# Seven block products in place of eight in the feed-forward layers of a three-layer fp32 stack

## The chip, the core and the metric

The kernel runs on one core of a Trainium2 chip. The metric is device time in microseconds (us) from the start to the end of one execution. Engines are named as in the profile: PE does matrix products (PEld is its weight load), DVE, ACT and POOL work on tiles elementwise, SP issues DMAs.

## The reference

512 tokens of width 1024 go through three layers in fp32. Two hybrid layers mix attention, a convolution and retention, and a third layer mixes differential attention with a state-space model. Each layer ends in a feed-forward part, and these are what is changed:

```
# hybrid layers (two of them): w_up 1024 x 4096, w_down 4096 x 1024
h = rms_norm(x, g_mlp_pre)
f = jnp.square(jax.nn.relu(h @ w_up)) @ w_down
x = x + rms_norm(f, g_mlp_post)
# last layer: w_up 1024 x 5632, w_down 2816 x 1024, conv of three tokens on each column
gate, val = split(causal_dwconv(h @ w_up), 2)
x = x + (silu(gate) * val) @ w_down
```

## The kernel before, in words

**Products.** PE has fp32r operands, so each fp32 operand is split in a high part (rounded to fp32r) and a low part (the rest), and each product is three matmuls: high x high, high x low, low x high (`mm3`, line 863; `t_part`, line 911). The high part of a weight chunk is a copy (`nc.copy`, ACT, or DVE at a planned penalty), the low part a subtraction (`nc.sub`, DVE or POOL).

**Weights** stream from memory in the order of `stream_spec` (line 60) in chunks of 128 x 1024 (512 KB). `Stream.load_to` loads a chunk into one of 4 raw slots (pool `wr`, tile wraw), and `prep_to` (line 748) makes the tiles whi and wlo of it in one of 4 slots each. `take` (line 766) hands a chunk to the products that use it. Preparation is wanted 15 us before use (`PREPV`).

**Feed-forward before.** The normed input lies transposed in hhi, hlo (features on partitions, 512 tokens as columns). The up projection makes one block of 128 hidden features per chunk: 8 x 3 matmuls with 512 columns (`f_unit`, line 890); the first four blocks of a layer are made in two halves of 256 tokens (`f_split`, line 896), since the second half of the input is still being normed. `relu2` (in `mlp`, line 1444), or the convolution and Silu (in `ffn2`, line 2006), takes each block out of PSUM and splits it in fhi, flo. The down projection (`down`, line 1483) takes four blocks of features at a time: for each half of the 1024 outputs it uses two chunks, for each of four tiles of 128 tokens 4 x 3 matmuls with 512 columns into one PSUM bank, which DVE adds to the accumulator acc (or to X in the last layer). Down group g-1 follows up group g. `finish_mlp` (line 1504) does the last group and the norms.

**Order.** The kernel records every instruction with the time by which it is wanted, and a planner (class `Trace`, line 400) orders them before anything runs, with a cost for each (`cost`, line 682: 1.04 ns a column and 65 ns for a DVE tensor_tensor, 2.1 ns a column and 150 ns for one on POOL). It simulates the engines as independent of each other. Where an instruction may go on two engines, it goes on the one where cost plus a bias ends first; in the feed-forward parts POOL's bias is -1000 ns (`wbias` 3). On the chip each engine then runs its list in that order. All instructions are issued by line 642, which is why the profile shows this line everywhere; they are told apart by their tiles. In the first feed-forward part a side task (`ssm_params`, line 1525) computes parameters of the third layer on POOL and DVE.

```python
    BIAS = [2000.0, 100000.0, -4449.0, -1000.0]                       # line 404
    def sub(self, out, a, b, bias=1):                                 # line 648
        alts = [("vector", "tensor_tensor", None)]
        if all(v.t.pool.space == "SB" for v in (out, a, b)):
            alts.append(("gpsimd", "tensor_tensor", bias))
```

PSUM has 4 banks for main products (`psp`) and 4 for side tasks (`pss`).

Of the kernel before, what the change touches and what calls it, by code (L numbers as in the profile page):

```python
# [46 lines left out]
def mlp_groups():  # L47
    return [(4 * g, 4) for g in range(NG1)]


def ffn2_groups():
    n = DFF2 // 128
    return [(k, min(4, n - k)) for k in range(0, n, 4)]
# [6 lines left out]
def stream_spec():  # L60
    out = []
    for l in range(LAYERS):
        for m in range(2):
            out.append(f_chunk("w_in", l, C_CONV + 128 * m))
            out.append(f_chunk("w_in", l, C_CONV + 256 + 128 * m))
        for c in (C_RV, C_RQ, C_RK, C_AV):
            out += t_chunks("w_in", l, ((c, 384),))
        for p in range(3):
            out.append(f_chunk("w_in", l, C_AQ + 128 * p))
            out.append(f_chunk("w_in", l, C_AK + 128 * p))  # L70
        for p in range(3):
# [3 lines left out]
        gs = mlp_groups()  # L75
        for g, (k0, n) in enumerate(gs):
            out += [f_chunk("w_up", l, 128 * (k0 + i)) for i in range(n)]
            if g:
                out += down_chunks("w_down", l, *gs[g - 1])
        out += down_chunks("w_down", l, *gs[-1])  # L80
# [19 lines left out]
    gs = ffn2_groups()  # L100
    for g, (k0, n) in enumerate(gs):
        for i in range(n):
            out.append(f_chunk("w_up_2", 0, 128 * (k0 + i)))
            out.append(f_chunk("w_up_2", 0, DFF2 + 128 * (k0 + i)))
        if g:
            out += down_chunks("w_down_2", 0, *gs[g - 1])
    out += down_chunks("w_down_2", 0, *gs[-1])
# [117 lines left out]
class View:  # L225
    """A view of a tile that is traced before the tile is placed."""
# [47 lines left out]
    def mask(self):  # L274
        """First and last column, and which ones between unless it's all."""
# [54 lines left out]
class DramView(View):  # L330
    """A view of a tile in DRAM: taken as a whole."""
# [20 lines left out]
class Pool:  # L352
    """Equal slots, which the order of instructions deals out to tiles. Each is a pool of one buffer."""
# [46 lines left out]
class Trace:  # L400
    """Records instructions with the time by which each is wanted, orders them, and issues them."""
# [246 lines left out]
    def sub(self, out, a, b, bias=1):  # L648
# [3 lines left out]
        return self.add(alts, (out, a, b), {"op": ALU.subtract})  # L652
# [119 lines left out]

class Side:
# [35 lines left out]
class Builder:  # L809
# [3 lines left out]
    NR, NW = 4, 4  # L813
# [6 lines left out]
    def __init__(self, tc, ctx, A, out):  # L820
# [17 lines left out]
        self.wbias = 2  # L838

# [23 lines left out]
    def mm3(self, ps, w, a, start, stop):  # L863
        nc = self.nc
        (whi, wlo), (ahi, alo) = w, a
        nc.tensor.matmul(ps, whi, ahi, start=start, stop=False)
        nc.tensor.matmul(ps, whi, alo, start=False, stop=False)
        nc.tensor.matmul(ps, wlo, ahi, start=False, stop=stop)
        self.tick(3 * ahi.n * 0.422)
# [72 lines left out]
    # ---------------------------------------------------------------- norms  # L942
# [42 lines left out]
    def to_hT(self, t, hs):  # L985
        nc = self.nc
        for h in range(2):
# [4 lines left out]
            self.split(ps.rearrange("p (k n) -> p k n", k=4), self.hhi[sl], self.hlo[sl])  # L992
# [66 lines left out]
    # ---------------------------------------------------------------- attention helpers  # L1059
# [41 lines left out]
    def v_pack(self, src):  # L1101
        """V of six heads, each as 64 columns of high parts and 64 of low parts."""
# [11 lines left out]
    def pv_pair(self, h, pts, V, y):  # L1114
        """One head's output, from the products with the high and the low parts of V below each other."""
# [19 lines left out]
    def rows(self, third):  # L1135
        """Room for the four rows of blocks of a lower triangle."""
# [3 lines left out]
    def p_split(self, parts):  # L1140
        """High and low parts by blocks of keys: 512, 384 and twice 256 columns, the last with a block of zeros."""
# [58 lines left out]
    # ---------------------------------------------------------------- conv module  # L1200
# [48 lines left out]
    # ---------------------------------------------------------------- retention  # L1249
# [87 lines left out]
    # ---------------------------------------------------------------- hybrid layer  # L1337
    def hybrid(self, l):
# [69 lines left out]
        # output projection and residual  # L1408
# [14 lines left out]
        self.side.drain()  # L1423
        self.finish(lambda t: (p0[t],), 4, W_OUT_KS, mix, X, gpost, gpre)
# [18 lines left out]
    # ---------------------------------------------------------------- MLP  # L1443
    def mlp(self, l, X):
        nc = self.nc
        groups = mlp_groups()
# [3 lines left out]
        acc = [None] * NT  # L1450
        f = {}
        last_g = len(groups) - 1

        def relu2(m):
            def ev(ps):
                r = self.s2()
                nc.vector.tensor_scalar(r, ps, 0.0, None, op0=ALU.max)
                hi, lo = self.s2(F32R, "fhi"), self.s2(F32R, "flo")
                nc.scalar.activation(hi, r, AF.Square)
                nc.scalar.activation(r, r, AF.Square)  # L1460
                nc.vector.tensor_tensor(lo, r, hi.bitcast(F32), op=ALU.subtract)
                f[m] = (hi, lo)
            return ev
        lhs = lambda k, t0, t1: tuple(z[:, t0:t1] for z in f[k])
        for g, (k0, n) in enumerate(groups):
            if g == 0:
                self.f_split([relu2(i) for i in range(n)], self.mid_start((1, 3)))
                gpost = self.load_gain(4 * l + 3)
                nxt = 4 * (l + 1) if l + 1 < LAYERS else 8
                gpre = self.load_gain(nxt)  # L1470
            else:
                for i in range(n):
                    self.f_unit(relu2(k0 + i))
                self.down(groups[g - 1], lhs, acc, f, g == 1)
        xd = [[self.dp.tile(F32, f"xd{l}_{t}_{h}", [P, 512]) for h in range(2)] for t in range(NT)]

        def store(t):
            for h in range(2):
                nc.sync.dma_start(out=xd[t][h], in_=X[t][h])
        self.finish_mlp(groups[-1], lhs, acc, X, gpost, gpre, store)  # L1480
        self.xd = xd

    def down(self, grp, lhs, acc, f, first):
        nc = self.nc
        k0, n = grp
        nch = n // 2
        ks = list(range(k0, k0 + n))
        for h in range(2):
            ws = [self.ws.take() for _ in range(nch)]
            for t in range(NT):  # L1490
                ps = self.ps()
                for c in range(nch):
                    self.t_part(ps, ws[c], ks[2 * c:2 * c + 2], t, 512, lhs, c == 0, c == nch - 1)
                if first:
                    if h == 0:
                        acc[t] = [None, None]
                    acc[t][h] = self.s2(name="acc")
                    nc.scalar.copy(acc[t][h], ps)
                else:
                    nc.vector.tensor_tensor(acc[t][h], ps, acc[t][h], op=ALU.add)  # L1500
        for k in ks:
            f.pop(k)

    def finish_mlp(self, grp, lhs, acc, X, gpost, gpre, store):
        nc = self.nc
        k0, n = grp
        nch = n // 2
        ks = list(range(k0, k0 + n))
        ws = [self.ws.take() for _ in range(2 * nch)]
        hs = {}  # L1510
        for t in range(NT):
            for h in range(2):
                ps = self.ps()
                for c in range(nch):
                    self.t_part(ps, ws[h * nch + c], ks[2 * c:2 * c + 2], t, 512, lhs, c == 0, c == nch - 1)
                nc.vector.tensor_tensor(acc[t][h], ps, acc[t][h], op=ALU.add)
            self.post_update(t, acc[t], X, gpost)
# [3 lines left out]
            store(t)  # L1521
        self.pending = hs

    # ---------------------------------------------------------------- SSM parameters
# [158 lines left out]
    # ---------------------------------------------------------------- SSM  # L1683
# [84 lines left out]
    # ---------------------------------------------------------------- differential attention  # L1768
# [84 lines left out]
    def second(self):  # L1853
# [139 lines left out]
        hs = {}  # L1993
        for t in range(NT):
# [11 lines left out]
    def ffn2(self, X):  # L2006
        nc = self.nc
        f, tg = {}, {}
        self.wbias = 3
        cw, cb = PV["convw2"][0], PV["convb2"][0]  # L2010

        def unit(i, val):
            c = i + (22 if val else 0)

            def ev(ps):
                t = self.s2(name="cv")
                w = [self.pvt[:, cw + 3 * c + j:cw + 3 * c + j + 1] for j in range(3)]
                nc.scalar.activation(t, ps, AF.Identity, scale=w[2], bias=self.pvt[:, cb + c:cb + c + 1])
                nc.vector.scalar_tensor_tensor(t[:, 1:], ps[:, :511], w[1], t[:, 1:], op0=ALU.mult, op1=ALU.add)
                nc.vector.scalar_tensor_tensor(t[:, 2:], ps[:, :510], w[0], t[:, 2:], op0=ALU.mult, op1=ALU.add)  # L2020
                if not val:
                    nc.scalar.activation(t, t, AF.Silu)
                    tg[i] = t
                else:
                    g = tg.pop(i)
                    nc.vector.tensor_tensor(t, t, g, op=ALU.mult)
                    hi, lo = self.s2(F32R, "fhi"), self.s2(F32R, "flo")
                    self.split(t, hi, lo)
                    f[i] = (hi, lo)
            return ev  # L2030
        lhs = lambda k, t0, t1: tuple(z[:, t0:t1] for z in f[k])
        groups = ffn2_groups()
# [47 lines left out]
```

## Time and profile before

| | |
|---|---|
| time, median of 3 runs | 2184.35 us (2183.29 to 2185.64) |
| span of the profiled execution, first to last instruction, which is its own time | 2185.0 us |
| PE busy | 2065.8 us (95%) |
| DVE, ACT, POOL busy | 1395.2, 928.5, 745.5 us |
| moved from and to memory | 204.25 MB read, 19.14 MB written |

Busy time of an engine is the union of its instructions; a waiting instruction that has already started counts as busy. Matmuls overlap in the records, so their distance in time from start to start is the price of one, not their duration. The same holds for DVE: one instruction's end overlaps the next one's start by about 0.1 us.

### The profile page before, as it was taken

To read this page: it belongs to the slowest core of one execution; us is meant where nothing else is said; L and a number is where in the kernel's file an instruction comes from. 1 tells how busy PE (TensorE), PEld (TensorE's weight loads), DVE (VectorE), ACT (ScalarE), POOL (GpSimd) and SP (SyncE) were. 2 spreads that over 40 slices of the span, in tenths; PEclk is the share of its full clock that TensorE was granted. 3 is DMA by queue.
4 is the path that set the end of the run, shared out by engine and by line. 5 is a ranking of instruction groups with operands and counts; after the bars stand their busy time and mean duration, and the time that the engine had idled before them with its cause. 6 is when DMAs were issued, how large, how long until landed. Compare 5 with 4: busy or idle time off the path is not lost. (4 is left out here: it accounts for less than half of the span.)

```text
span 2185.0 us, 27033 instructions
## 1 busy us (share of the span) xinstructions
PE 2065.8 (95%) x9964; PEld 1711.6 (78%) x9964; DVE 1395.2 (64%) x2131; ACT 928.5 (42%) x1521; POOL 745.5 (34%) x858
## 2 busy tenths in 40 slices
PE   7789989899999799989999998999999999999999
PEld 7777878778888777788888877677777788888887
DVE  6999596344457999573444464379888646655545
ACT  3267544232234267454222344456578324433332
POOL 3663357980004663210000115764643431000000
PEclk9999999999999999999999999999999999999999
DMA  5223233332333224133332346222224533333222
GB/s 176 80 78 123 87 116 109 128 127 87 97 114 97 87 68 135 49 107 97 96 97 77 115 133 201 79 80 68 92 82 135 169 96 97 97 96 97 87 87 77
DMA packets 85556, 225.16 MB, mean 103 GB/s; under 512 B 10416, under 2 KB 20400, under 8 KB 85424
## 3 DMA queue, kind: packets, MB, share of 16 engines
q1 hardware_dynamic: 85424, 223.43, 32.4%
q8 instruction: 79, 1.29, 0.3%
q14 instruction: 53, 0.43, 0.1%
HBM read 204.25 MB, written 19.14 MB: 102 GB/s over the span
## 5 line engine op out<-in xcount | busy, mean ns | idle before, releaser
L642 POOL TENSOR_TENSOR wlo<-wraw,whi 128x1024 fp32r<-128x1024 f32 (+1 forms) x156 | 374.5, 2408 | 1068.3 <-ACT whi L642 824.9
L642 ACT CAST whi<-wraw 128x1024 fp32r<-128x1024 f32 (+1 forms) x323 | 330.4, 1029 | 726.7 <-PE ps L642 592.1
L642 PE MATMUL ps<-hhi,whi 128*128 128x512 f32 (+1 forms) x1488 | 506.8, 370 | 7.3 <-DVE acc L642 3.1
L642 PE MATMUL ps<-hlo,whi 128*128 128x512 f32 (+1 forms) x1488 | 504.8, 370 | 5.6 <-DVE hlo L642 5.6
L642 PE MATMUL ps<-hhi,wlo 128*128 128x512 f32 (+1 forms) x1488 | 504.3, 369 | 0.3 <-DVE wlo L642 0.3
L642 PEld LDWEIGHTS ps<-hhi,whi 128*128 128x128 f32 x1488 | 272.4, 191 | 54.8 <-issue 4.0
L642 PEld LDWEIGHTS ps<-hlo,whi 128*128 128x128 f32 x1488 | 272.4, 191 | 53.5 <-DVE hlo L642 6.8
L642 PEld LDWEIGHTS ps<-hhi,wlo 128*128 128x128 f32 x1488 | 272.1, 191 | 48.2 <-DVE wlo L642 1.0
L642 DVE TENSOR_TENSOR wlo<-wraw,whi 128x1024 fp32r<-128x1024 f32 x178 | 223.4, 1257 | 114.8 <-ACT whi L642 114.5
L642 PE MATMUL ps<-whi,fhi 128*128 128x512 f32 x688 | 249.7, 392 | 6.1 <-DVE t L642 3.7
L642 PE MATMUL ps<-whi,flo 128*128 128x512 f32 x688 | 249.5, 391 | 0.0
L642 PE MATMUL ps<-wlo,fhi 128*128 128x512 f32 x688 | 249.5, 391 | 0.0
L642 PE MATMUL ps<-wlo,hhi 128*128 128x384 f32 (+1 forms) x448 | 162.7, 380 | 18.3 <-POOL wlo L642 18.1
L642 DVE TENSOR_TENSOR acc<-ps,acc 128x512 f32<-128x512 f32 x112 | 76.5, 687 | 154.7 <-PE ps L642 154.7
L642 PE MATMUL ps<-whi,hhi 128*128 128x384 f32 (+1 forms) x448 | 161.7, 383 | 14.2 <-DVE rotb L642 12.7
L642 PE MATMUL ps<-whi,hlo 128*128 128x384 f32 (+1 forms) x448 | 158.8, 377 | 0.0
L642 PEld LDWEIGHTS ps<-whi,fhi 128*128 128x128 f32 x688 | 129.6, 189 | 34.7 <-DVE t L642 4.2
L642 PEld LDWEIGHTS ps<-wlo,fhi 128*128 128x128 f32 x688 | 129.6, 189 | 27.8
L642 PEld LDWEIGHTS ps<-whi,flo 128*128 128x128 f32 x688 | 129.5, 188 | 27.8
L642 DVE SCALAR_TENSOR_TENSOR cacc<-cy,pv,cacc 128x509 f32<-128x509 f32 (+26 forms) x120 | 125.3, 1088 | 0.6
L642 POOL TENSOR_TENSOR st<-st,mhalf 128x1 f32<-128x1 f32 (+1 forms) x56 | 54.9, 981 | 194.4 <-DVE st L642 190.8
L642 PEld LDWEIGHTS ps<-wlo,hhi 128*128 128x128 f32 x448 | 86.9, 195 | 30.6 <-POOL wlo L642 21.6
(250 smaller groups left out, 3167.8 us busy)
## 6 DMA issues: line engine op xcount, KB each, us to landing
wraw<-in_wst SPq DMA_DIRECT2D x302, 512.0 KB, 3.5
wraw<-in_wst SPq DMA_DIRECT2D x32, 384.0 KB, 3.1
gain<-in_gains SPq DMA_DIRECT2D x20, 256.0 KB, 4.2
X<-in_x SPq DMA_DIRECT2D x16, 256.0 KB, 6.1
xd<-X SPq DMA_DIRECT2D x16, 256.0 KB, 2.0
X<-xd SPq DMA_DIRECT2D x16, 256.0 KB, 4.9
gated<-t SPq DMA_DIRECT2D x16, 256.0 KB, 2.4
gate<-gated SPq DMA_DIRECT2D x16, 256.0 KB, 3.7
```

The lines of the kernel that those rows point to most:

```text
L642: getattr(getattr(self.nc, e), m)(*[r(x) for x in op.args], **{k: r(v) for k, v in op.kw.items()})
```

## The change

In each feed-forward part, all but the first four feature blocks of the up projection and the last group of the down projection are computed by 2 x 2 blocks with seven block products (Strassen's algorithm in Winograd's form). Tokens are cut in halves of 256, the inner dimension and the outputs in halves too. A unit takes two chunks x, y of 128 x 1024, and makes 84 matmuls of 256 columns (7 products of 4 x 3). Before, two chunks made 48 matmuls of 512 columns.

- The sums of weight blocks are made on chip: `take_fast` makes four sums of 512 columns (into a third raw slot, tile wsum, in place of y, and into a tile of the common pool) and splits 3.5 chunks instead of 2.
- The sums of the activations are made on chip: `fast_in` once a layer for the input, `fast_mid` for each pair of hidden feature blocks.
- The block products are combined by `FastUp.out` and `FastDown.out`, as they leave PSUM. Each unit uses two PSUM banks; products 4 and 3 of a unit run within the next unit.
- X is written to memory before the layer and read back at its end. whi and wlo get 5 slots each in place of 4, the common pool 51 tiles of 128 x 512 in place of 55.

There are 14 up and 14 down units in each hybrid layer, and 20 up and 10 down units in the last, 86 in all. The planner, its costs and its biases are as before.

```diff
+    def take_fast(self):
+        x, y = self.raw.pop(j), self.raw.pop(j + 1)
+        t0 = b.T - b.PREPV
...
+        b.prio(t0)
+        split(x, (1, 2))
+        b.prio(t0 + 3 * b.PROD)
+        z, z4 = b.wr.tile(name="wsum"), b.s2(name="wsum")
+        nc.sum(z[:, L], x[:, L], y[:, L], b.wbias)
+        nc.sum(z[:, R], z[:, L], y[:, R], b.wbias)
+        split(z, (5, 6))
+        b.prio(t0 + 6 * b.PROD)
+        nc.sum(y[:, L], y[:, L], y[:, R], b.wbias)
+        nc.sum(z4, z[:, R], x[:, R], b.wbias)
+        split(y, (7, 3))
+        b.prio(t0 + 8 * b.PROD)
+        split(z4, (4,))
...
+    def fast_mid(self, g0, g1, s4, e):
+        sa = self.s2(name="sraw")
+        nc.sub(sa[:, R], g0[:, R], g1[:, R], self.wbias)
+        nc.sub(sa[:, L], sa[:, R], g0[:, L], self.wbias)
+        nc.sum(s4[0][:, H], g1[:, L], sa[:, L], self.wbias)
+        nc.sub(g0[:, R], g0[:, L], g0[:, R], self.wbias)
+        for src, names in ((g0, (1, 7)), (g1, (2, 4)), (sa, (6, 5))):
+            hi, lo = self.s2(F32R, "fhi"), self.s2(F32R, "flo")
+            nc.copy(hi, src)
+            nc.sub(lo, src, hi.bitcast(F32), self.wbias)
...
+        hi, lo = s4[1][:, H], s4[2][:, H]
+        nc.copy(hi, s4[0][:, H])
+        nc.sub(lo, s4[0][:, H], hi.bitcast(F32), self.wbias)
...
+class FastUp(Fast):
+    def out(self, i):
+        pa, pb = self.pa[:, :256], self.pb[:, :256]
+        if i == 1:
+            nc.copy(m0[:, L], pa)
+        elif i == 2:
+            nc.vector.tensor_tensor(g0[:, L], pb, m0[:, L], op=ALU.add)
+        elif i == 6:
+            nc.copy(m0[:, R], pa)
+        elif i == 7:
+            nc.copy(m1[:, L], pa)
+            nc.vector.tensor_tensor(g1[:, R], pb, m1[:, L], op=ALU.subtract)
+        elif i == 4:
+            nc.copy(g0[:, R], pa)
+            self.done(0, g0)
+        elif i == 3:
+            nc.vector.tensor_tensor(g1[:, L], pb, m0[:, R], op=ALU.subtract)
+            self.done(1, g1)
...
+class FastDown(Fast):
+    def out(self, i):
+        if i in (1, 6, 7):
+            m = b.s2(name="mid")
+            nc.copy(m, pa)
...
+                nc.sub(C[1, 1], C[1, 1], m, b.wbias)
+        elif i == 2:
...
+                V(C[0, 0], pb, C[0, 0], op=ALU.add)
+                nc.sum(C[0, 0], C[0, 0], self.m1, b.wbias)
+        elif i == 5:
+                V(C[1, 1], pb, C[1, 1], op=ALU.add)
+        elif i == 4:
+                V(C[1, 0], pa, C[1, 0], op=ALU.add)
+        elif i == 3:
+                V(C[0, 1], pb, C[0, 1], op=ALU.add)
+                nc.sub(C[0, 1], C[0, 1], self.mu, b.wbias)
...
-    NR, NW = 4, 4
+    NR, NW = 4, 5
+    PROD = 1300
...
+    def fast_unit(self, u):
+        for i in (1, 2, -4, 6, -3, 5, 7):
...
+        def done(j):
+            def d(e, g):
+                nc.vector.scalar_tensor_tensor(g, g, 0.0, g, op0=ALU.max, op1=ALU.mult)
```

In the last layer `conv(i, val, src)` reads the combined block from SBUF, where it read PSUM before, with the same instructions.

## Rows read from the trace of the kernel before

**Rows 1.** The page: its head, and the first of its busy lines.
```profile
span 2185.0 us, 27033 instructions
PE 2065.8 (95%) x9964; PEld 1711.6 (78%) x9964; DVE 1395.2 (64%) x2131; ACT 928.5 (42%) x1521; POOL 745.5 (34%) x858
```
**Rows 2.** The chain that ended last: start us, us, what (of six pieces one).
```profile
1819.57 361.70 PE ps L642 x1640
```
**Rows 3.** Busy by stretch: stretch us, its length, engines' busy us, PEclk, DMA share, GB/s.
```profile
50.00:100.00 50.00, 37.21 (x189) 35.17 (x188) 49.96 (x68) 8.80 (x16) 27.25 (x19) 0.90 0.26 82
985.00:1250.00 265.00, 265.00 (x1153) 216.28 (x1153) 116.81 (x130) 83.51 (x104) 16.67 (x8) 1.00 0.31 93
1860.00:2150.00 290.00, 290.00 (x1255) 235.57 (x1255) 158.22 (x190) 100.73 (x126) 9.66 (x4) 1.00 0.30 95
```
**Rows 4.** Timeline of PE in the second layer's f_split: start us, us, instruction.
```profile
962.02 0.28 PE L642 MATMUL ps<-hhi,wlo 128*128 128x256 f32 x1
...
963.38 0.28 PE L642 MATMUL ps<-hhi,wlo 128*128 128x256 f32 x1
```
**Rows 5.** Timeline of PE in the second layer's down projection.
```profile
1046.11 0.39 PE L642 MATMUL ps<-whi,fhi 128*128 128x512 f32 x1
...
1047.47 0.39 PE L642 MATMUL ps<-whi,fhi 128*128 128x512 f32 x1
```
**Rows 6.** Timeline of DVE in the same feed-forward part, two stretches.
```profile
1023.62 0.69 DVE L642 TENSOR_SCALAR t<-ps 128x512 f32<-128x512 f32 x1 [13.73 <-PE ps L642]
1024.23 1.21 DVE L642 TENSOR_TENSOR wlo<-wraw,whi 128x1024 fp32r<-128x1024 f32 x1
1026.16 2.10 DVE L642 TENSOR_TENSOR flo<-t,fhi 128x512 fp32r<-128x512 f32 x1 [0.71 <-ACT t L642]
1028.18 1.21 DVE L642 TENSOR_TENSOR wlo<-wraw,whi 128x1024 fp32r<-128x1024 f32 x1
...
1050.80 1.22 DVE L642 TENSOR_TENSOR wlo<-wraw,whi 128x1024 fp32r<-128x1024 f32 x1 [1.08 <-ACT whi L642]
1051.94 0.68 DVE L642 TENSOR_TENSOR acc<-ps,acc 128x512 f32<-128x512 f32 x1
```
**Rows 7.** Timeline of POOL beside the first stretch of rows 6.
```profile
1025.06 2.65 POOL L642 TENSOR_TENSOR wlo<-wraw,whi 128x1024 fp32r<-128x1024 f32 x1 [66.40 <-PE ps L642]
```
**Rows 8.** Timelines of POOL and of DVE in the first layer's mixing part.
```profile
61.38 8.28 POOL L642 TENSOR_TENSOR wlo<-wraw,whi 128x768 fp32r<-128x768 f32 x4
...
60.65 3.51 DVE L642 SCALAR_TENSOR_TENSOR cacc<-cy,pv,cacc 128x501 f32<-128x501 f32 x2
64.09 3.87 DVE L642 TENSOR_TENSOR vhl<-rvt,vhl 128x256 fp32r<-128x256 f32 x2
...
75.82 1.38 DVE L642 SCALAR_TENSOR_TENSOR cacc<-cy,pv,cacc 128x497 f32<-128x497 f32 x2
```
**Rows 9.** Timelines of POOL and of DVE in the first feed-forward part.
```profile
376.50 3.38 POOL L642 TENSOR_TENSOR wlo<-wraw,whi 128x1024 fp32r<-128x1024 f32 x1
...
378.71 0.69 DVE L642 TENSOR_SCALAR t<-ps 128x512 f32<-128x512 f32 x1 [1.08 <-PE ps L642]
```
**Rows 10.** POOL's groups by shape, whole run: count | busy us, mean ns | idle before.
```profile
L642 POOL TENSOR_TENSOR wlo<-wraw,whi 128x1024 fp32r<-128x1024 f32 x124 | 307.4, 2484 | 1037.8 <-ACT whi L642 794.7 <-PE ps L642 144.4 <-DVE cv L642 64.4
L642 POOL TENSOR_TENSOR z<-z,ct 128x512 f32<-128x512 f32 x8 | 10.3, 1286 | 9.1 <-ACT wsw L642 9.1
```
**Rows 11.** Busy by stretch for the tile t alone (columns as in rows 3).
```profile
330.00:480.00 150.00, 0.00 (x0) 0.00 (x0) 22.96 (x50) 16.43 (x26) 123.72 (x341) 0.97 0.34 111
```
**Rows 12.** ACT's groups by shape, second feed-forward part, 985 to 1250 us.
```profile
L642 ACT CAST whi<-wraw 128x1024 fp32r<-128x1024 f32 x48 | 49.9, 1051 | 162.0 <-PE ps L642 161.9
L642 ACT ACTIVATE t<-t 128x512 f32<-128x512 f32 x24 | 15.2, 633 | 0.8
L642 ACT COPY acc<-ps 128x512 f32<-128x512 f32 x8 | 4.7, 585 | 17.4 <-PE ps L642 17.4
```
**Rows 13.** The page's DMA issues: KB each, us from issue to landing.
```profile
wraw<-in_wst SPq DMA_DIRECT2D x302, 512.0 KB, 3.5
xd<-X SPq DMA_DIRECT2D x16, 256.0 KB, 2.0
X<-xd SPq DMA_DIRECT2D x16, 256.0 KB, 4.9
```

More of the change, by code (lines that the diff above doesn't have):

```diff
@@ L44, with mlp_plan, ffn2_plan, fast_down @@
 W_OUT_KS = (3, 4, 0, 1, 5, 6, 7, 2)
[L47 to L53, printed above, removed]
+NF2 = DFF2 // 128
+def mlp_plan():
+    out = []
+    for g in range(NG1 - 1):
+        last = g == NG1 - 2
+        out.append(("up", 2 * g + 2, 0))
+        if last:
+            out.append(("up", 2 * g + 3, 0))
+        out += [("down", g, 0), ("down", g, 1)]
+        if not last:
+            out.append(("up", 2 * g + 3, 0))
+    return out
+def ffn2_plan():
+    out = [("up", 2, 0), ("up", 3, 0)]
+    n = NF2 // 4
+    for g in range(n):
+        i = 4 * g + 4
+        out.append(("up", i, 0))
+        if g == n - 1:
+            out.append(("up", i + 1, 0))
+        out += [("down", g, 0), ("down", g, 1)]
+        if g < n - 1:
+            out += [("up", i + e, 0) for e in range(1, 4)]
+    return out
+def fast_down(name, l, g, nb):
+    ks = (4 * g, 4 * g + 2, 4 * g + 1, 4 * g + 3)
+    return [(name, l, ks, ((512 * nb + 256 * e, 256),)) for e in range(2)]
 GATES = (2, 3, 4, 7)
@@ L99, in stream_spec @@
         out += t_chunks("w_out_2", 0, ((512 * h, 512),))
[L100 to L107, printed above, removed]
+    up2 = lambda i: [f_chunk("w_up_2", 0, DFF2 * e + 128 * i) for e in range(2)]
+    out += up2(0) + up2(1)
+    for kind, i, nb in ffn2_plan():
+        out += up2(i) if kind == "up" else fast_down("w_down_2", 0, i, nb)
+    out += down_chunks("w_down_2", 0, NF2 - 2, 2)
     return out
@@ new lines, with __init__, run, mm @@
+class Fast:
+    FIRST = {1, 2, 5}
+    def __init__(self, b, w, a):
+        self.b, self.w, self.a = b, w, a
+        self.pa, self.pb = b.ps(), b.ps()
+    def run(self, i):
+        self.mm(i, self.pa if i in (1, 6, 7, 4) else self.pb, i in self.FIRST)
+        self.b.evac(self.out, i)
+        if i in (2, 3):
+            self.pb = self.pb if i == 2 else None
+class FastUp(Fast):
+    def __init__(self, b, w, a, done):
+        super().__init__(b, w, a)
+        self.done = done
+        self.g = [b.s2(name="cu") for _ in range(2)]
+        self.m = [b.s2(name="mid") for _ in range(2)]
+    def mm(self, i, ps, first):
+        whi, wlo = (x.rearrange("p (k m) -> p k m", k=4) for x in self.w.pop(i))
+        for k in range(4):
+            self.b.mm3(ps[:, :256], (whi[:, k, :], wlo[:, k, :]), self.a(i, k), first and k == 0, k == 3,
+                       skip_group_check=not first)
+    def out(self, i):
+        nc, (g0, g1), (m0, m1) = self.b.nc, self.g, self.m
+        pa, pb = self.pa[:, :256], self.pb[:, :256]
+        L, R = slice(0, 256), slice(256, 512)
+        if i == 1:
[13 more added lines that the diff above has]
+            self.done(1, g1)
@@ L994, in run, with fast_s4, fast_end @@
+    def fast_s4(self):
+        return self.s2(name="sraw"), self.s2(F32R, "fhi"), self.s2(F32R, "flo")
+    def fast_unit(self, u):
+        v = self.before
+        for i in (1, 2, -4, 6, -3, 5, 7):
+            if i > 0:
+                u.run(i)
+            elif v:
+                v.run(-i)
+        self.before = u
+    def fast_end(self):
+        for i in (4, 3):
+            self.before.run(i)
+        self.before = None
     def run(self):
@@ L1441, in finish, with spill @@
         self.pending = hs
+    def spill(self, X, name):
+        out = [[self.dp.tile(F32, f"{name}_{t}_{h}", [P, 512]) for h in range(2)] for t in range(NT)]
+        for t in range(NT):
+            for h in range(2):
+                self.nc.sync.dma_start(out=out[t][h], in_=X[t][h])
+        return out
     def mlp(self, l, X):
         nc = self.nc
-        groups = mlp_groups()
         self.wbias = 3
@@ L1464, in mlp @@
[L1464 to L1470, printed above, removed]
-            else:
-                for i in range(n):
-                    self.f_unit(relu2(k0 + i))
-                self.down(groups[g - 1], lhs, acc, f, g == 1)
+                f[m] = r
@@ L2007, in ffn2, with conv @@
         nc = self.nc
-        f, tg = {}, {}
         self.wbias = 3
+        xm = self.spill(X, "xm2")
+        del X
+        f, ops, s4, C, tg = {}, {}, {}, {}, {}
         cw, cb = PV["convw2"][0], PV["convb2"][0]
-        def unit(i, val):
+        def conv(i, val, src):
             c = i + (22 if val else 0)
[L2015 to L2030, printed above, removed]
@@ new lines, in ffn2 @@
+        us = [lambda ps, i=i, v=v: conv(i, v, ps) for i in range(2) for v in (False, True)]
+        self.f_split(us, self.mid_start((1, 3)))
+        a = self.fast_in()
+        for kind, i, nb in ffn2_plan():
+            w = self.ws.take_fast()
+            if kind == "up":
+                self.fast_unit(FastUp(self, w, a, lambda e, g, i=i: conv(i, e, g)))
+            else:
+                self.fast_unit(self.fast_down(w, ops, C, i, nb))
+        self.fast_end()
+        X = []
+        for t in range(NT):
+            X.append([self.s2(name="X") for _ in range(2)])
+            for h in range(2):
+                nc.sync.dma_start(out=X[t][h], in_=xm[t][h])
+                for j in range(2):
+                    sl = slice(256 * j, 256 * j + 256)
+                    part = C[t // 2, j, h][:, (t % 2) * 256:(t % 2) * 256 + 256]
+                    nc.sum(X[t][h][:, sl], X[t][h][:, sl], part, self.wbias)
```

264 lines of the change are left out of this document (200 added, 64 removed).

## The prediction

> **What bounds the kernel now.** Read the page's head first: PE is busy 95% of 2185.0 us [rows 1]. Then the chain that ended last: its last 361.70 us are 1640 matmuls and nothing else, so the last layer's feed-forward part is pure PE [rows 2]. The stretches show the same of the second and third feed-forward parts: PE has no gap (265.00 of 265.00 us, 290.00 of 290.00), DVE is busy 44% and 55%, ACT a third, POOL hardly [rows 3]. What I need next is the price of a matmul. Twelve starts of 256 columns lie between 962.02 and 963.38, 0.1133 us each [rows 4]; six of 512 columns between 1046.11 and 1047.47, 0.2267 us each [rows 5]. So half the columns cost exactly half, each with its own weight load, and PE has all it needs to gain from smaller blocks. The last thing to see is the price of an elementwise instruction and who gets in its way, below.
>
> **PE's part.** A unit is 84 x 0.1133 = 9.52 us after, 48 x 0.2267 = 10.88 us before. Over 86 units that is 936 us before and 819 after: **117 us less**, if nothing else binds. The remaining matmuls of these parts are untouched.
>
> **DVE's prices.** From start to start, DVE took 1.14 us for a subtraction of 1024 columns (1050.80 to 1051.94) and 0.61 for 512 columns (1023.62 to 1024.23) [rows 6]. The slope between them gives 0.34 for 256, an estimate from these two. A scalar_tensor_tensor with a pointer of 500 columns took 1.38 - 0.73 = 0.65, the two of one row less one's length [rows 8].
>
> **What the units ask of DVE and POOL.** I count instructions whose two inputs lie in SBUF (S) apart from those that read PSUM (Q).
> - Weights, each unit: three subtractions of 1024, one of 512, four sums of 512: 3 x 1.14 + 5 x 0.61 = 6.47 S. Before: 2 x 1.14.
> - Up unit, hybrid layers: three instructions out of PSUM (1.02 Q), two relu-squares (1.22 S), `fast_mid` with four sums of 256, three subtractions of 512 and one of 256 (3.53 S). Together 11.22 S, 1.02 Q.
> - Down unit: four adds out of PSUM (2.44 Q), three adds in SBUF (1.83 S): 8.30 S, 2.44 Q.
> - Up unit, last layer: four convolution steps, now on SBUF (2.60 S), a product (0.61), half of `fast_mid` (1.77): 11.45 S, 1.02 Q.
>
> Means: 9.76 S and 1.73 Q in the hybrid layers (as many up as down), 10.40 S and 1.49 Q in the last (two up to one down). DVE alone would need 11.49 and 11.89 us for a unit, where PE needs 9.52 and a unit took 10.88. So POOL must help, and the sum hangs on whether it can.
>
> **What POOL's help costs.** At 1026.16 a subtraction on DVE of 0.69 us took 2.10: POOL had one running from 1025.06 to 1027.71, and DVE's ended 0.55 us after that [rows 6, 7]. Where both have a queue, they take turns: in 61.38 to 69.66 four POOL subtractions and four DVE instructions alternate, and none of DVE's ends before the POOL one that it met [rows 8]. An instruction that reads PSUM goes free: 0.69 us at 378.71, inside a POOL subtraction [rows 9]. So S work on DVE and S work on POOL is done one after the other. POOL takes 2.48 us for 1024 columns and 1.29 for 512 [rows 10], 2.1 times DVE's price. Each us that POOL works therefore saves DVE 0.48 and blocks it for 1.00.
>
> The Trainium skill has this as a rule that speaks against the change: "SBUF — State Buffer", section "Who interferes with whom", says that a DVE instruction with two SBUF inputs and a GpSimd instruction that reads SBUF exclude each other for the whole instruction, and that one with a PSUM input doesn't take part. By that rule, the rows agree, the exclusion holds for all S work and not for these tiles alone.
>
> **How much the planner gives to POOL.** Its costs take the engines as independent and prefer POOL by 1000 ns. For 512 columns POOL ends by its count after 1225 - 1000 = 225 ns, DVE after 597, so a free POOL gets it; for 1024 it is 1300 against 1130, and POOL gets it when DVE is more than 170 ns behind. Before, DVE was idle half the time and POOL got next to nothing (16.67 us of 265) [rows 3]. Now DVE is behind nearly always. Where both are kept at work the load of 11.5 us on 9.52 is about 0.8 of what two independent engines could do, so I take POOL planned at 0.8 of a unit, 7.6 us, which is 3.6 us of DVE's price. Bounds: 0.5 (work often not ready when POOL is free, with four raw slots of which a unit holds three) and 0.95 (never without work).
>
> **The sum.** S work in line, PSUM work beside POOL's:
> - second feed-forward part: 9.76 - 3.6 + 7.6 = 13.8 us a unit, 28 units: 385 us
> - last: 10.40 - 3.6 + 7.6 = 14.4, 30 units: 432 us
> - first: the side task's POOL instructions (tile t, 123.7 us [rows 11]) stand in the same line. POOL planned at 0.9 of 266 us is 240: 124 for the side task, 116 for the change, worth 55 of DVE: 273 - 55 + 116 + 124 = 458 us
>
> Together 1275 us against 936: **+339**. `fast_in` adds 16 S instructions of 512 columns (9.8 us) at the start of each part; half of it hides beside `f_split`, whose second half holds PE for 10.9 us: +5 each, +15. The end of the last layer adds 5 us of sums on X, mostly beside matmuls: +5. Sum: 2185 + 339 + 20 = 2544; the median of the runs is 0.65 below the profiled execution, so **2543, say 2540**.
>
> Edits at nothing, and their cover. ACT: 3.5 casts a unit at 1.05 and 0.63, four copies out of PSUM below 0.59 each, four splits at 0.63: at most 8.6 us [rows 12], under 13.8; if S were faster than 8.6, ACT would bind next. Weight traffic: the same 1 MB a unit, in more time. Spill and reload of X: 16 DMAs of 256 KB a part on SP's queue, landing after 2.0 and 4.9 us [rows 13]; the weight loads queue behind the stores, whose wait is X, ready before `f_split` ends; the cost is between nothing and 8 x 2 us a part, and I take nothing, since preparation, not arrival, is late. The fifth whi slot is not what is short: it buys room, not S time. PSUM: products 4 and 3 of the unit before lie between 1 and 6, so PE has 2.7 us for an emptied bank; when DVE is blocked it waits longer, but PE has 4 us of slack in each unit by then.
>
> **The unknowns.** The exclusive time of a POOL instruction may be a little below its record: four of 768 columns at 2.48 x 0.75 = 1.86, with DVE's 0.55 + 0.65 + 0.34 + 0.2 between them, make 9.2 us, and the rows show 8.28 [rows 8], a tenth less. On the other side, lists fixed in advance run late against each other, and both engines may stand; the rows show that they need not, and I bound it by a tenth. I let the two cancel. By the ends: POOL at 0.5 gives 343 + 387 + 402 = 1132, +196 and 20, 2400 us; POOL at 0.95 gives 406 + 453 + 465 = 1324, and a tenth on it 1456, +520 and 20, 2725.
>
> **Rivals.**
> 1. *The engines do add up* (faster). If S work ran on both at once, 11.5 us of load would fit in 9.52 us and PE would bind: 2185 - 117 + 20 = **2088**. It decides where a unit falls below 10.88 us. For it: PE's and the products' part is sound, and DVE's PSUM work does run free [rows 9]. Against: rows 6 to 8. Chance 0.04.
>  The Trainium skill's "Perfetto Trace Analysis", section "Optimizing Scalar/DVE Operations", advises to move work off a saturated DVE, even to GpSimd, and warns that between these two it might not help. By its advice the time would be this rival's, by its warning, which rows 6 to 8 bear out, the forecast's.
> 2. *POOL gets little after all*, as before, and DVE bears it alone: 56 x 11.49 + 30 x 11.89 = 1000 us, +64 and 20: **2270**; with the side task in line 2390. For it: the planner left POOL idle in these parts. Against: DVE had slack then. Chance 0.13, of which 0.01 lies at no change.
> 3. *The three raw slots close a loop.* y of the next unit can load only when x is free, which is after three sums one behind the other: 3.5 us to land [rows 13], then three sums, each behind POOL and DVE instructions. If each waits for two of POOL's (2.6 us) and one of DVE's (1.14) and takes 1.29, the loop is 3.5 + 3 x 5.0 = 18.5 us, and 86 units give 2185 + 655 = **2840**. A colder PE would add to this: the granted clock was 0.90 where PE was busy 37 of 50 us [rows 3], that is, some of the time at 1.2 GHz in place of 2.4. Chance 0.08.
>
> That seven products aren't seven or cost more on PE is excluded by the diff and rows 4 and 5.
>
> **Numbers.** Forecast 0.75, rivals 0.04, 0.13 and 0.08. A measurement of this kernel can tell about 0.2% from no change. Faster 0.04, same 0.01, slower 0.95. The forecast's own range is 2400 to 2725; cutting the thin upper end and most of the rivals, the 8 in 10 range is 2390 to 2700.
>
> **What would show it.** Right: in the stretches of the three feed-forward parts PE falls to about 0.7 of the time, DVE to nine tenths and more with POOL at half or more; DVE's two-SBUF groups have means far above 1.22 and 0.69, those with PSUM their old 0.69; PE's idle time is released by tiles wlo, wsum and flo; matmuls of 256 columns still start every 0.113 us where they run. Wrong: POOL below a fifth (rival 2), PE above 95% in these parts (rival 1), or DVE and POOL both idle behind DMA (rival 3).

## The result and the profile after

The changed kernel takes 2530.61 us, against 2184.99 of the kernel before on the same chip: ratio 1.157, 95% interval 1.155 to 1.159. Three executions took 2528.04 to 2531.00 us; a fourth, slow one of 8753.84 us is left out of the ratio. The forecast was 2540, its range 2390 to 2700. The profiled execution spans 2528.5 us. First the head of the page and its busy lines, against [rows 1]:

```profile
span 2528.5 us, 35458 instructions
PE 2129.6 (84%) x13060; PEld 1908.1 (75%) x13060; DVE 2059.7 (81%) x2683; ACT 1203.4 (48%) x2081; POOL 1648.4 (65%) x1388
```

PE's busy time, the union of its records, rose by 64 us although fewer columns pass through it; part of its matmuls now run at a lower clock (below). Its share of the span fell from 95% to 84%, while DVE gained 664 us of busy time and POOL 903. In the chain that ended last, [rows 2] was one piece of 361.70 us of matmuls. After, the same view of the changed kernel can follow only the last 110 us, in 106 pieces such as these (start us, us, what):

```profile
2419.12 9.52 PE ps L667 x65
...
2434.87 2.11 POOL cv L667
2436.97 1.68 POOL wsum L667
2438.65 1.68 POOL sraw L667
...
2452.65 2.89 DVE wlo L667 x2
```

The end is no longer set by one engine alone: between short runs of matmuls the chain goes through DVE and POOL, which hand it to each other. The busy time by stretch (columns as in rows 3) of the three feed-forward parts, each taken from the end of the output projection to its last down product, and of the stretch in the second part used below for all comparisons:

```profile
302.00:814.00 512.00, 391.37 (x2677) 369.56 (x2676) 426.78 (x558) 206.12 (x345) 435.90 (x517) 0.87 0.27 90
1104.00:1548.00 444.00, 368.35 (x2677) 350.02 (x2677) 389.09 (x404) 207.22 (x347) 333.29 (x203) 0.93 0.28 93
2052.00:2524.00 472.00, 385.13 (x2774) 367.63 (x2774) 424.64 (x401) 226.38 (x367) 351.44 (x210) 0.91 0.23 75
1150.00:1400.00 250.00, 209.32 (x1525) 200.38 (x1525) 218.32 (x211) 111.71 (x176) 194.69 (x117) 0.92 0.23 76
```

In the second and last part, where PE had no gap [rows 3], it stands 17 and 18% of the time, in the first 24%. Its granted clock is 0.87 to 0.93, where rows 3 had 1.00 for the second and last part: some matmuls now run at 1.2 GHz in place of 2.4. DVE is busy 83 to 90%, POOL 74 to 85%. Yet the records of both are long because each waits inside them for the other. Some eight microseconds of the second part, in the timeline of POOL and then of DVE:

```profile
1320.69 1.71 POOL L667 TENSOR_TENSOR flo<-cu,fhi 128x512 fp32r<-128x512 f32 x1
1322.37 1.18 POOL L667 TENSOR_TENSOR sraw<-cu,sraw 128x256 f32<-128x256 f32 x1
1323.51 1.73 POOL L667 TENSOR_TENSOR wsum<-wsum,wraw 128x512 f32<-128x512 f32 x1
```

```profile
1321.21 1.75 DVE L667 TENSOR_TENSOR flo<-cu,fhi 128x512 fp32r<-128x512 f32 x1
1322.88 1.22 DVE L667 TENSOR_TENSOR flo<-sraw,fhi 128x512 fp32r<-128x512 f32 x1
1324.02 1.77 DVE L667 TENSOR_TENSOR wraw<-wraw 128x512 f32<-128x512 f32 x1
1325.71 1.75 DVE L667 TENSOR_TENSOR wlo<-wraw,whi 128x1024 fp32r<-128x1024 f32 x1
1327.38 0.41 DVE L667 TENSOR_TENSOR cu<-ps,mid 128x256 f32<-128x256 f32 x1
1327.71 0.68 DVE L667 TENSOR_TENSOR acc<-ps,acc 128x512 f32<-128x512 f32 x1
```

POOL's three end at 1322.40, 1323.55 and 1325.24, DVE's first three at 1322.96, 1324.10 and 1325.79: each 0.55 or 0.56 us behind one of POOL's, the time by which DVE's subtraction in rows 6 ended behind the one of row 7. They take turns as in rows 8; the means of the groups below say that this is common. The two last, reading PSUM, have their old lengths.

That the line of two-SBUF work is full can be added up. Groups by shape from 1150 to 1400 us, DVE's largest and then POOL's:

```profile
L667 DVE TENSOR_TENSOR wlo<-wraw,whi 128x1024 fp32r<-128x1024 f32 x29 | 56.3, 1943 | 3.5 <-ACT whi L667 3.5
L667 DVE SCALAR_TENSOR_TENSOR cu<-cu 128x512 f32<-128x512 f32 x18 | 28.7, 1631 | 0.0
L667 DVE TENSOR_TENSOR wlo<-wsum,whi 128x1024 fp32r<-128x1024 f32 x17 | 22.3, 1310 | 8.3 <-ACT whi L667 8.3
L667 DVE TENSOR_TENSOR acc<-ps,acc 128x512 f32<-128x512 f32 x27 | 17.8, 677 | 0.0
```

```profile
L667 POOL TENSOR_TENSOR wsum<-wsum,wraw 128x512 f32<-128x512 f32 x21 | 39.2, 1868 | 2.0 <-DVE wsum L667 1.3
L667 POOL TENSOR_TENSOR acc<-acc,mid 128x512 f32<-128x512 f32 x21 | 39.0, 1859 | 6.5 <-DVE acc L667 5.2
L667 POOL TENSOR_TENSOR wlo<-wraw,whi 128x1024 fp32r<-128x1024 f32 x9 | 22.6, 2509 | 9.6 <-ACT whi L667 8.8 <-PE ps L667 0.8
```

Over all such groups DVE has 46 two-SBUF instructions of 1024 columns, 80 of 512 and 25 of 256, at the prediction's prices 46 x 1.14 + 80 x 0.61 + 25 x 0.34 = 110 us. POOL has 9, 82 and 26: by rows 10 and their slope 9 x 2.48 + 82 x 1.29 + 26 x 0.69 = 146 us. Together 256 us in a stretch of 250: one line, full. DVE's subtraction of 1024 columns on wraw has gone from 1.2 us to 1.94 apiece; what reads PSUM has stayed at 0.68.

Last, what PE waits for in the second part (waits: us in total, times, longest us):

```profile
PE ps L667 <- ACT mid L667: 23.9, 19, 2.6
PE ps L667 <- DVE cu L667: 14.8, 10, 2.9
PE ps L667 <- ACT fhi L667: 10.0, 8, 5.6
PE ps L667 <- DVE acc L667: 6.7, 6, 1.5
PE ps L667 <- POOL flo L667: 5.6, 5, 1.1
```

Mostly it waits for a PSUM bank to be emptied (mid, cu, acc), and less for operands (fhi, flo). DVE empties cu and acc, and does so behind the blocked instructions of its list. ACT empties mid, and its list stands before casts whose input DVE and POOL make late (the same view of ACT, three of its lines):

```profile
ACT fhi L667 <- DVE cu L667: 49.0, 21, 3.6
ACT whi L667 <- DVE wsum L667: 46.5, 16, 4.8
ACT whi L667 <- POOL wsum L667: 33.7, 14, 4.1
```

### The profile page after: what moved, and what is told of

It reads as the page before. It is cut to its first block, busy times and chain, and to the rows that moved or that the text cites. A ratio compares the mean times of both kernels' runs of the same rounds, so it can differ in the third digit from the quotient of the medians.

```text
span 2528.5 us, 35458 instructions
## 1 busy us (share of the span) xinstructions
PE 2129.6 (84%) x13060; PEld 1908.1 (75%) x13060; DVE 2059.7 (81%) x2683; ACT 1203.4 (48%) x2081; POOL 1648.4 (65%) x1388
## 5 line engine op out<-in xcount | busy, mean ns | idle before, releaser
L667 POOL TENSOR_TENSOR wlo<-wraw,whi 128x1024 fp32r<-128x1024 f32 (+1 forms) x172 | 422.5, 2464 | 366.7 <-ACT whi L667 243.4
L667 PE MATMUL ps<-hhi,whi 128*128 128x256 f32 (+1 forms) x1488 | 439.5, 325 | 73.0 <-ACT mid L667 41.8
L667 PE MATMUL ps<-hlo,whi 128*128 128x256 f32 (+1 forms) x1488 | 433.4, 321 | 12.1 <-DVE hlo L667 11.2
L667 PE MATMUL ps<-hhi,wlo 128*128 128x256 f32 (+1 forms) x1488 | 432.9, 320 | 0.0
L667 PE MATMUL ps<-whi,fhi 128*128 128x256 f32 (+1 forms) x1144 | 323.8, 314 | 97.4 <-ACT mid L667 39.8
L667 PE MATMUL ps<-whi,flo 128*128 128x256 f32 (+1 forms) x1144 | 311.0, 308 | 22.6 <-DVE flo L667 11.8
L667 PE MATMUL ps<-wlo,fhi 128*128 128x256 f32 (+1 forms) x1144 | 312.1, 306 | 5.8 <-POOL wlo L667 5.8
L667 PE MATMUL ps<-shi,whi 128*128 128x256 f32 (+1 forms) x608 | 188.8, 315 | 66.1 <-DVE cu L667 61.1
L667 ACT CAST whi<-wsum 128x1024 fp32r<-128x1024 f32 (+1 forms) x172 | 142.0, 834 | 194.9 <-DVE wsum L667 98.7
L667 PE MATMUL ps<-slo,whi 128*128 128x256 f32 (+1 forms) x608 | 182.1, 304 | 0.0
L667 PE MATMUL ps<-shi,wlo 128*128 128x256 f32 (+1 forms) x608 | 181.5, 304 | 0.2 <-DVE wlo L667 0.2
## 6 DMA issues: line engine op xcount, KB each, us to landing
wraw<-in_wst SPq DMA_DIRECT2D x302, 512.0 KB, 3.3
```

The costliest lines, as they stand in the source:

```text
L667: getattr(getattr(self.nc, e), m)(*[r(x) for x in op.args], **{k: r(v) for k, v in op.kw.items()})
```

## The experiments

Two theories stood against each other after the result. **A**: the two-SBUF instructions of DVE and POOL exclude each other, and POOL's help costs more than it brings. **B**: the work is simply too much, or the order of it or the buffers bind, and POOL's help is needed. The table gives the length of each feed-forward part (from PE's timeline, bounds as above, in us), the whole time, and the ratio to the kernel before on the chip of the same run (2184.99 to 2185.29 us).

| kernel | first | second | last | time | ratio, 95% interval |
|---|---|---|---|---|---|
| before | 379.6 | 363.0 | 368.8 | 2184.99 | 1 |
| after | 512.0 | 444.0 | 472.8 | 2530.61 | 1.157 [1.155, 1.159] |
| e1 POOL's help off | 471.1 | 376.4 | 399.4 | 2346.33 | 1.074 [1.072, 1.076] |
| e2 sums left out | 390.8 | 352.2 | 355.1 | 2197.11 | 1.005 [1.003, 1.008] |
| e3 up units alone | 401.7 | 349.5 | 351.1 | 2199.02 | 1.006 [1.005, 1.008] |
| e4 four whi slots | 501.6 | 445.2 | 476.5 | 2490.43 | 1.140 [1.137, 1.142] |
| e5 e1, POOL reads | 471.2 | 457.1 | 403.3 | 2425.52 | 1.110 [1.108, 1.112] |
| e6 e1, POOL writes | 471.4 | 378.4 | 399.5 | 2344.58 | 1.073 [1.071, 1.075] |
| e7 up units, two parts | 381.3 | 347.5 | 357.6 | 2157.26 | 0.987 [0.986, 0.989] |
| e8 bias 2000 | 469.4 | 378.4 | 397.4 | 2341.31 | 1.071, one execution, no interval |

**e1: POOL's help off.** The bias against POOL goes from -1000 to 100000 ns in the feed-forward parts, so that DVE does all the two-SBUF work of the units.

```diff
-        self.wbias = 3
+        self.wbias = 1
```

> The changed kernel with POOL forbidden for all subtractions and sums of the feed-forward parts (the side task stays on POOL). Theory (work with two SBUF inputs on DVE and on POOL runs one after the other, and POOL is 2.1 times slower): taking POOL's help away makes the kernel FASTER. DVE alone needs 11.49 us a unit in the hybrid layers and 11.89 in the last, 322 and 357 us for the second and third parts, where the changed kernel took about 353 and 410 for the units; with the side task's 124 us in line, some 400 in the first. Total about 2370 us, between 2310 and 2430. Rival (the engines do add up, and the time is lost elsewhere, as in the loop of the raw slots or in PE's clock): DVE then carries all the load that two engines carried, so 2530 us or more.

Taking an engine's help away made the kernel 184 us faster, as theory A expected (2310 to 2430). Busy by stretch, and then two of DVE's groups in it:

```profile
1150.00:1400.00 250.00, 226.92 (x1846) 220.50 (x1845) 247.12 (x391) 129.35 (x209) 0.00 (x0) 1.00 0.30 103
```

```profile
L667 DVE TENSOR_TENSOR wlo<-wraw,whi 128x1024 fp32r<-128x1024 f32 x44 | 52.7, 1218 | 0.0
L667 DVE TENSOR_TENSOR wsum<-wsum,wraw 128x512 f32<-128x512 f32 x43 | 29.4, 684 | 0.0
```

In 250 us DVE alone, busy 99%, gets 1846 matmuls fed, where both got 1525 fed. Its instructions are back at their clean lengths, and PE's clock at 1.00. DVE is what binds: by PE's timeline the 28 units of the second part take 322.7 us from first to last product, 11.5 each, where the prediction worked out 11.49 for DVE alone.

**e5 and e6: does POOL's reading block DVE, or its being busy?** Both are e1 with idle POOL work on a tile of its own in each unit of the second part: in e5 four adds that read SBUF, in e6 ten memsets that only write.

```diff
+                for _ in range(4):
+                    nc.gpsimd.tensor_tensor(idle, self.cm[:, :S], self.cm[:, :S], op=ALU.add)
```

```diff
+                for _ in range(10):
+                    nc.gpsimd.memset(idle, 0.0)
```

> The kernel of e1 (POOL forbidden for the feed-forward parts' work, 2346 us) with four additions of 512 columns more on POOL in each of the 28 units of the second part; they read a constant and write a tile that nobody else uses, so no instruction waits for them. POOL is idle there otherwise; they are 4 x 1.29 = 5.2 us of its time a unit, 144 us in all. Theory (an instruction of DVE with two SBUF inputs and one of POOL that reads SBUF exclude each other): DVE, which is busy 49 of 50 us there, loses what POOL works, less what lies beside its PSUM work (1.7 us a unit): the second part grows by 80 to 130 us. Rival (independent engines): by less than 5 us.

> As e5, with ten memsets of 512 columns a unit in place of the four additions: about as much of POOL's time (0.42 us for 384 columns in the trace of before), but POOL only writes. If it is the reading of SBUF that excludes, the second part grows by less than 10 us; if any work of POOL on SBUF does, by 80 us or more as in e5.

The same stretch of e5, and groups of DVE and POOL in it:

```profile
1150.00:1400.00 250.00, 202.54 (x1537) 194.41 (x1538) 246.37 (x326) 109.53 (x174) 78.61 (x55) 0.92 0.22 76
```

```profile
L667 DVE TENSOR_TENSOR wlo<-wraw,whi 128x1024 fp32r<-128x1024 f32 x37 | 51.9, 1419 | 0.0
L667 DVE TENSOR_TENSOR acc<-ps,acc 128x512 f32<-128x512 f32 x31 | 20.7, 679 | 0.0
L667 POOL TENSOR_TENSOR idle<-cm 128x512 f32<-128x512 f32 x55 | 79.6, 1447 | 4.3
```

And of e6:

```profile
1150.00:1400.00 250.00, 226.90 (x1833) 220.49 (x1831) 245.81 (x388) 127.94 (x207) 71.05 (x135) 0.99 0.29 103
```

```profile
L667 DVE TENSOR_TENSOR wlo<-wraw,whi 128x1024 fp32r<-128x1024 f32 x44 | 52.6, 1216 | 0.0
L667 POOL MEMSET idle<- 128x512 f32 x135 | 71.1, 527 | 7.8
```

POOL is busy for 79 and 71 of the 250 us, nearly alike. Its adds lengthen the second part by 80.7 us over e1, at the lower edge of the 80 to 130 expected, its memsets by 2.0. The 112 adds at 1.29 are 144 us of POOL; DVE's PSUM work, 28 x 1.73 = 48 us, doesn't mind them, which leaves up to 96. So the exclusion is shown as a cause: by reading, not by being busy, and not for instructions on PSUM (0.679 us). The Trainium skill, "SBUF — State Buffer", section "Who interferes with whom", says just this: a DVE instruction with two SBUF inputs contends with a GpSimd instruction that reads SBUF and not with one that only writes it. The two runs agree.

**e4: four whi slots.** The fifth weight slot, which the change had taken from the common pool of tiles, goes back to it (`NR, NW = 4, 5` becomes `4, 4`).

> The changed kernel with four slots for whi and wlo in place of five, which gives the common pool its 55 tiles back. It asks where the 26 us come from that the mixing parts lost in the changed kernel (7 us before the first output projection, 7 in it, 14 in the second layer). If the smaller common pool is the cause, the mixing parts of this kernel are as before (first output projection starts at 235 us, ends at 287) and the total falls by up to 26 us, to about 2505; if the copies for the feed-forward part that follows are the cause, they stay, and the total with them at 2530. By the theory of the exclusion the units themselves change little, as the fifth slot buys room and no time: the second part stays within 15 us of 444.

The kernel got 40 us faster, more than the 26 expected. The feed-forward parts stayed within 4 us of the changed kernel's in the second and last part and gained 10 in the first; 35 us came from the mixing parts. Before, these three took 287.5, 275.3 and 506.7 us; in the changed kernel 302.2, 289.6 and 503.7, together 26 more; in e4 285.3, 273.6 and 501.3, 9 less than before. The first mixing part by stretch, of the changed kernel and then of e4:

```profile
10.00:280.00 270.00, 230.48 (x1203) 201.92 (x1203) 223.78 (x339) 133.65 (x246) 125.33 (x128) 0.92 0.29 96
```

```profile
10.00:280.00 270.00, 241.66 (x1282) 210.53 (x1282) 224.83 (x372) 137.41 (x260) 132.69 (x136) 0.97 0.31 105
```

e4 has the 1282 matmuls of the kernel before, the changed kernel 1203, with the same instructions to do. So the fifth slot costs where no line of the units was touched. The slot and the four tiles of the common pool change hands together, and no run takes the tiles away alone: that the smaller pool is what costs is likely, and not shown.

**e2: the sums left out.** Seven products, but the operands' sums on chip are not made (their places take other operands). With them go the splits of the weight sums and of sa and s4, half of them casts on ACT, and the third raw slot. It asks for the price of the sums, and what PE gains without them.

```diff
-        nc.sum(z[:, L], x[:, L], y[:, L], b.wbias)
-        nc.sum(z[:, R], z[:, L], y[:, R], b.wbias)
-        split(z, (5, 6))
...
-        nc.sum(y[:, L], y[:, L], y[:, R], b.wbias)
-        nc.sum(z4, z[:, R], x[:, R], b.wbias)
...
-        split(z4, (4,))
+        out[5], out[6], out[4] = out[7], out[3], out[1]
...
-        nc.sub(sa[:, R], g0[:, R], g1[:, R], self.wbias)
-        nc.sub(sa[:, L], sa[:, R], g0[:, L], self.wbias)
-        nc.sum(s4[0][:, H], g1[:, L], sa[:, L], self.wbias)
-        nc.sub(g0[:, R], g0[:, L], g0[:, R], self.wbias)
```

> The changed kernel without the sums of weight blocks and of hidden feature blocks: products 4, 5 and 6 use the tiles of other products again, so the output is another one, but all matmuls, all evacuations of PSUM, the split of both chunks and of both feature blocks, the spill of X and the sums of the layer's input stay. Work with two SBUF inputs falls from 9.8 to about 4.0 us a unit. Theory: PE binds again, with 9.52 us a unit, 117 us less than before, and the starts of the parts and the mixing parts (some 26 us longer in the changed kernel) stay: 2115 us, between 2085 and 2150. Rival (the order of the seven products, the emptying of two PSUM banks in turn, or the matmuls of 256 columns cost PE what they save): 2185 us or more, with PE waiting for ACT and DVE at PSUM though both have time to spare.

A miss by 82 us, into the rival's range, and a useful one. That it lies 334 us below the changed kernel says that the sums and their splits together were the cost; it does not part DVE and POOL from ACT or the raw slots, as e1, e5 and e6 do. But PE did not gain 117 us. The three parts by stretch:

```profile
301.30:692.10 390.80, 345.65 (x2678) 336.88 (x2677) 251.88 (x393) 152.49 (x262) 269.53 (x432) 0.94 0.36 118
982.70:1334.90 352.20, 336.43 (x2678) 327.56 (x2679) 227.74 (x273) 152.85 (x264) 127.96 (x83) 0.99 0.37 119
1836.10:2191.20 355.10, 341.34 (x2776) 333.28 (x2775) 240.62 (x274) 172.22 (x289) 144.62 (x95) 1.00 0.31 101
```

PE is busy 96% of the second and last part, so there it binds again, but its matmuls cost more than forecast. In its timeline of the second part 2464 of 2544 starts of 256 columns lie below 0.126 us apart, 0.118 on the mean; rows 4 had 0.1133. At 0.118 a unit is 9.9 us, not 9.52: 34 us over the 86 units. PE also stands, for 45 us in the first part, where the side task is in the line too, and for 16 and 14 in the others; its waits for banks of PSUM, of which the rival made the cause, are below 9 us in each of these two. The longer mixing parts are no part of the miss, since the 2115 has them in it. Why 256 columns cost more was not tried and stays open.

**e3: up units alone.** Seven products in the up projections; the down projections as before. It is e1 with the plan of weights and the down loop of the kernel before (the two lines of the plan stand for the rest).

```diff
-        for kind, i, nb in mlp_plan():
+        for g in range(1, NG1):
...
+            self.down((4 * (g - 1), 4), lhs, acc, f, g == 1)
```

> Seven products in the up projections alone, the down projections as before, and POOL forbidden for the weights of the feed-forward parts. A part asks of DVE, up and down in turn, 9.9 and 4.7 us a unit, on the mean 7.3 us where PE needs 10.2. Theory: PE binds, 48 units save 1.36 us each, 65 us; 20 us of starts and 26 us of longer mixing parts are taken off that: about 2165 us, between 2140 and 2195; the first part, with the side task's 124 us of POOL in line, saves the least. Rival (seven products cost time beyond DVE's and POOL's line, in PSUM or in the raw slots): half of the loss of the changed kernel, 2300 us or more.

Just outside the expectation (2195 at most). The second part gains 13.5 us on the kernel before, the last 17.7; the first, with the side task's POOL work, loses 22, and the mixing parts, with five slots as in the changed kernel, lose some 25. Both losses can be taken out:

**e7: up units alone, in the second and last part, with four whi slots.** The first part is that of the kernel before.

> Seven products in the up projections of the second and third part alone; the first part (where the side task's 124 us of POOL stand in line) and all down projections as before; POOL forbidden for the second and third part's weights; four slots for whi and wlo and 55 common tiles. From e3 and e4: the second part gains 13.5 us and the third 17.7 against before, the mixing parts are as before or 4 us shorter. Theory: 2150 us, between 2140 and 2165, faster than both kernels. Rival (what e3 gained there hangs on its longer mixing parts or its smaller pool): 2180 us or more.

As expected (2140 to 2165), this beats both kernels: 0.987 of the time before. Stretches of its second and its last part:

```profile
1000.00:1250.00 250.00, 250.00 (x1586) 226.35 (x1585) 176.53 (x242) 100.41 (x150) 0.67 (x2) 1.00 0.36 114
1880.00:2100.00 220.00, 216.22 (x1467) 198.17 (x1466) 184.90 (x268) 117.41 (x180) 0.00 (x0) 1.00 0.31 102
```

PE is without a gap again in the second part and at 98% in the last, with DVE at 71 and 84% and POOL idle. Here the line has room, and the seven products pay: 15.5 us in the second part and 11.2 in the last.

**e8: a bias of 2000 ns**, meant as a dose of POOL's help between e1 and the changed kernel (`wbias` 0, in the same two places as e1).

> The changed kernel with the planner's bias for POOL in the feed-forward parts at +2000 ns in place of -1000: POOL gets an instruction when DVE is far behind alone. A dose between the changed kernel (2531 us, POOL at work some 40 of 50 us in the second part) and e1 (2346, none). Theory: each us that POOL works costs about half a us, so the second part lies between e1's 376 us and the changed kernel's 444 in proportion to POOL's time; total between 2360 and 2500. Rival (POOL helps where it is really wanted): below e1's 2346.

The planner gave POOL nothing in the second and last part (0.00 us busy from 1150 to 1400, as in e1), so the run repeats e1 and says nothing of a dose. Its 2341 us, outside the 2360 to 2500 expected, is one execution 5 us below e1, and does not bear out the rival.

## Why the prediction was right, and where its terms were off

**The bound.** Right: two-SBUF work of DVE and POOL is one line (timelines, 256 us in 250, e5 against e6), and it binds in place of PE. Rival 1 (2088) fell to the same evidence, rival 3 (2840) too: DVE and POOL are busy, not standing behind DMA. Rival 2 is a kernel that could be built, e1. Its DVE-alone time is the prediction's mechanism with POOL at zero: 11.5 us a unit in the second part where 11.49 was worked out, 12.0 in the last where it was 11.89. Its 2346 us lie between that rival's 2270 and the 2390 with the side task in line.

**The sum by parts.** The table has the units of each part alone, in us, from their first product to their last by PE's timeline. "Line" is the two-SBUF work that ran between the two, counted by shape at the prediction's prices: DVE, POOL, and in the first part the side task's 124.

| part | units: forecast, measured | line | a unit: forecast, measured | a unit before: taken at, measured |
|---|---|---|---|---|
| first | 458, 451 | 192 + 171 + 124 | 16.4, 16.1 | 10.88, 11.57 |
| second | 385, 387 | 166 + 222 | 13.8, 13.8 | 10.88, 11.08 |
| last | 432, 434 | 192 + 247 | 14.4, 14.5 | 10.88, 11.10 |

In the second and last part the forecast came out for its own reason: the line is as long as the part. POOL was taken at 7.6 us a unit and did 7.9 and 8.2. In the first part there is luck in it. POOL did 171 us for the change where 116 were taken, and the line, 487 us, is longer than the 451 that passed. Two groups of the side task on POOL, in the kernel before, suggest why:

```profile
L642 POOL TENSOR_TENSOR t<-t,prm 128x256 f32<-128x256 f32 x32 | 22.4, 710 | 0.2
L642 POOL TENSOR_TENSOR t<-t,prm 128x16 f32<-128x16 f32 x32 | 7.9, 258 | 1.0
```

A sixteenth of the columns takes over a third of the time, so most of a short record can hardly be reading. That such instructions hold the line for less than their record is argued from this, and was not tried by itself.

**What failed.** Two terms of the sum, and they cancel. The first is what the units took before, 936 us. The 10.88 us come from six starts of a fast moment [rows 5]; rows 3 have the mean, 265.00 / 1153 x 48 = 11.03 and 290.00 / 1255 x 48 = 11.09. In the first part PE also stood at times before the change. The stretches of the units before:

```profile
320.00:644.00 324.00, 315.77 (x1358) 256.20 (x1357) 158.96 (x257) 100.29 (x126) 148.07 (x351) 0.98 0.36 113
972.00:1282.00 310.00, 310.00 (x1356) 253.24 (x1355) 142.33 (x171) 99.33 (x125) 16.67 (x8) 1.00 0.32 97
1837.00:2170.00 333.00, 333.00 (x1445) 270.75 (x1445) 184.06 (x221) 115.30 (x145) 12.06 (x5) 1.00 0.29 90
```

Together they are 967 us, so the units grew by 304 us and not by 339. The second term is "The fifth whi slot is not what is short: it buys room, not S time", which stood among the edits at nothing: the mixing parts grew by 26 us, and give them back without the slot (e4). Starts and ends of the parts were put at 20 us and took 13. So 2185 + 304 + 13 + 26 = 2528, where the forecast added 339 and 20. That the total came as near as 0.4% is luck; that the units came within 2% in each part is, but for the first, the mechanism.

**Steps that were off without deciding.** "So half the columns cost exactly half" does not hold on the mean: 0.118 us (e2) against 0.230 for 512 columns (265.00 / 1153), so PE's gain at best is 86 x (48 x 0.230 - 84 x 0.118) = 97 us, not 117, hidden here since PE doesn't bind. "PE's idle time is released by tiles wlo, wsum and flo": it is released by mid, cu and acc first, and wsum holds it up through ACT's list. PE stands 17 to 24%, not the 30% of "about 0.7"; its colder clock fills part of what would have been gap.

## What to carry to other kernels

Before work is moved to vector engines to spare TensorE, count it in two purses: what reads PSUM, and what reads two tiles in SBUF; the second is one purse for DVE and POOL together, and POOL draws 2.1 times as much from it for the same instruction. Where it is full, a planner that takes the engines as independent does harm, and giving POOL nothing is better (2346 against 2531 us). Strassen's seven products pay where the sums fit into that purse beside the rest: in the up projections alone, where no side task runs, they gave 1.3% (e7). And take the price of what is replaced from a long stretch, not from its fastest moment.

## What was not expected of the hardware

- Matmuls of one size do not all start at the same distance with PE full. In e2 from 1050 to 1100 us, 256 columns have a median of 0.116 to 0.118 us on hhi and hlo and of 0.120 on shi, slo, fhi and flo; in the kernel before, 512 columns take 0.2267 in rows 5 and 0.230 on the mean of rows 3. The cause is open.
- POOL's memsets, 71 us in 250, cost DVE's two-SBUF instructions nothing (1216 ns against 1218 without), where 79 us of adds in the same stretch left 1537 matmuls of 1846.
